# A squared-ReLU MLP's down pass: four row operands with stored low parts, four loaded later, one block between sum and square

## The chip, the cores and the metric

The kernel runs on one core of a Trainium2 chip. The metric is device time in microseconds (us) of one execution, and the number reported is the median of several runs. In what follows PE is TensorE, DVE is VectorE, ACT is ScalarE, POOL is GpSimd and SP is SyncE. SP and POOL each issue DMA transfers here, in the order in which they stand in that engine's program.

## The reference, cut to what matters

One layer of a decoder with attention, a convolution module and an MLP is computed for 512 prompt rows and 64 sample rows, 576 rows in all. The change lies in the MLP and touches its neighbours:

```
x    = x + concat(attn, conv) @ w_out                 # 2048 features
hid  = square(relu(rms_norm(x, g_mlp) @ w_up))        # 2048 -> 8192
x    = x + hid @ w_down                               # 8192 -> 2048
gate = sigmoid(rms_norm(x, g_ple) @ w_ple_gate)       # 2048 -> 2048
y    = rms_norm(x + (pe @ w_ple) * gate, g_final)
```

All of it is float32, with each row's norm taken over its 2048 features. The sum over the 8192 hidden features in `hid @ w_down` may be taken in any order.

## The kernel before

**Two stages.** The first, some 1000 us, computes the input projection, attention, convolution and output projection (`phase1`, the matmuls of line 493). The second is `phase2`, which works through three products one after another: the *up pass* (g = 1, `w_up`), the *down pass* (g = 2, `w_down`) and the *gate* (g = 3 to 5, `w_gate`). Features lie on partitions and rows on the free axis. A *row group* is 256 features of all 576 rows, so the input of the up pass and of the gate has 8 row groups and the hidden layer has 32.

**A block.** The up and down passes use a seven-product scheme for 2x2 blocks: a row group is kept as seven half-width operands (288 rows each; three are pieces of the data, four are sums `T` of them), a weight block as seven 128x128 operands, and seven products in seven PSUM banks are combined into a result afterwards. Each operand is split into a high part in the fast float32 type and a low part, the rest; each product then takes three matmuls (lines 1547 to 1549: high by high, high by low, low by high). So one *block*, one row group against one *part* of 256 output features, is 21 matmuls. The up pass has 32 parts of 8 blocks (blocks 0 to 255), the down pass 8 parts of 32 blocks (256 to 511). The down pass cuts each part's 32 blocks into several rounds: the first round takes the first 3, 3, 3, 4, 5, 6, 7 and 8 row groups for parts 0 to 7 (`DOWN_FIRST`), and each later round 7 or fewer. A part that isn't in its last round is added to DRAM by an accumulating DMA (line 1363).

**Row operands.** They live in a ring of eight slots (`xs`), each with seven high and seven low operands. When the last block that uses a slot is emitted, `mk` (line 1459) makes the next one: `load` issues on POOL's queue the DMA of the 1008 KB that a row group has in DRAM (`down_in`, in traces `di`, for the down pass; line 1470), and `build` then splits it in the slot: ACT copies it to the high part (`split_hi`, line 149), DVE subtracts (`split_lo`, line 152), in two pieces of 128x864 and 128x1152. All eight slots of the up pass are used until its last part, so slots 0 to 7 of the down pass are made during blocks 247 to 254 and first used in blocks 256, 257, 258, 268 (the last one of the fourth part's first round), 273, 279, 286 and 294. In the gate a slot holds row groups in another form, split by lines 1484 to 1486 (`xs<-xs,vecs`).

**Weights.** SP loads two blocks' weights in 512 KB (`w2r`, four buffers). For each block DVE forms sums of them (lines 1770 to 1772), ACT makes the high part (`w2h`, line 149) and DVE the low part (`w2l`, line 152), two blocks ahead of PE, with three buffers each.

**The end of a part.** ACT and DVE empty the seven banks and combine them (`combine_head`, lines 1663 to 1666, and `combine_tail`, lines 1676 to 1679). Then a generator finishes the part: `fin_up` multiplies by the row norm's scale on DVE, takes relu and square on ACT (lines 1354, 1355), forms the sums `T` on DVE and stores the row group to `down_in` on POOL's queue (lines 1311 to 1313); `fin_down` adds a partial part to DRAM or, in a part's last round, adds the residual on DVE (line 1366), stores it, and has ACT square it (line 1280) and DVE add the squares up for the next norm (line 1287). After the last part `norm` sums over partitions on PE (line 179), runs a chain of short DVE operations to 1/sqrt, puts them on a diagonal (`dg`, lines 183 and 185), spreads them by PE (line 189) and copies them to `rb` on ACT (line 190).

**What sets the order.** Each engine executes its instructions in the order in which the program emits them. The generators (finishing of parts in queue 0, builds of slots in queue 1, the last up part's finish in queue 2) are held by `Beside`. After each block `run` lets them emit as much as fits in the block's 2.79 us by their own estimate: a generator yields the cost of what it emitted, or a negative number, -n, to be passed over for n blocks. `flush` emits what is left of a generator at once where its result is needed. So a `yield -1` between two lines sets in the program one more block's weight work between the two, on every engine. Buffers of tag `b` (128 x 1152, `buf`, line 1268) hold `T`, squares, residuals and the diagonal; there are two of them.

## Time and profile before

| | |
|---|---|
| median of 3 runs | 2713.27 us (2712.22 to 2721.72) |
| profiled execution | 2715.1 us, span 2713.3 us |
| PE busy | 2658.0 us, 98% of the span, 21873 matmuls |
| DVE busy | 2044.1 us, 75% |
| ACT busy | 1151.2 us, 42% |
| POOL busy | 513.5 us, 19% |
| DMA | 536.12 MB, mean 198 GB/s |

The profiled execution took 2715.1 us from the host's view and 2713.3 us between its first and last record, so 1.8 us lie around the span. It is within the three runs' range. In the profile, the first matmul of the up pass starts at 1016.2 us of the span, the first of the down pass at 1742.8 us and its last at 2481.8 us; the gate follows. PE's busy time counts a matmul from its start to its modelled end, and matmuls overlap; what tells whether PE lost time in a stretch is the number of matmuls that it started there. The granted clock beside a stretch is 1.00 where PE had its full clock.

### The profile page before, as it was taken

The page shows a single profiled execution, that of the slowest core. Times are in us where ns is not written, and L with a number is a line of the kernel's source. Part 1 is how long each engine was busy: PE and PEld are TensorE (multiplying, and loading weights), DVE is VectorE, ACT ScalarE, POOL GpSimd, SP SyncE. Part 2 cuts the span into 40 slices and gives each one's busy share as a digit, 9 for nine tenths or more (in the row PEclk, how much of TensorE's full clock was granted, in tenths as well). Part 3 has the DMA queues.
Part 4 walks back from the last instruction along what each step waited for, and adds up shares of the span by engine and source line. Part 5 has one row for each costly group of instructions (what it writes and reads, how often), then busy time and mean ns, then how long its engine had stood idle before and what let it go on. Part 6 is the DMA issues. An engine that isn't in the chain of part 4 may idle for free.

```text
span 2713.3 us, 56293 instructions
## 1 busy us (share of the span) xinstructions
PE 2658.0 (98%) x21873; PEld 2569.6 (95%) x21873; DVE 2044.1 (75%) x3553; ACT 1151.2 (42%) x1692; POOL 513.5 (19%) x906
## 2 busy tenths in 40 slices
PE   9999999999999999999999999999999999998997
PEld 8899999888989998999999999999999999998997
DVE  6577777646554448888888888898888888897676
ACT  5222232235443325444444444454444444444554
POOL 2287786611000000000000000100000000000110
PEclk9999999999999999999999999999999999999998
DMA  5598898899754545444444444666565656655675
GB/s 203 176 302 295 299 297 294 286 308 319 242 202 149 175 168 171 155 142 142 142 140 141 142 143 140 233 149 174 164 189 155 182 154 179 177 183 186 192 241 172
DMA packets 238382, 536.12 MB, mean 198 GB/s; under 512 B 25537, under 2 KB 26562, under 8 KB 238114
## 3 DMA queue, kind: packets, MB, share of 16 engines
q1 hardware_dynamic: 170978, 327.86, 38.0%
q0 software_dynamic: 33600, 143.70, 16.9%
q10 hardware_dynamic: 33536, 60.96, 6.8%
q8 instruction: 171, 2.80, 0.4%
q14 instruction: 97, 0.79, 0.1%
HBM read 441.47 MB, written 90.96 MB: 196 GB/s over the span
## 4 chain that ended last, share of the span: by engine, by line
PE 55%; DVE 3%; issue 1%; ACT 1%; DVEq 0%; ACTq 0%
PE P L1548 16%; PE P L1547 16%; PE P L1549 16%; PE P L1616 2%; PE P L1617 2%; PE P L1615 2%; DVE w2l L152 1%; ACT w2h L149 0%; DVE xs L152 0%; DVE w2r L1771 0%; DVE w2r L1770 0%; DVE w2r L1772 0%; DVE x L1603 0%; DVE c L1664 0%; DVE c L1679 0%
## 5 line engine op out<-in xcount | busy, mean ns | idle before, releaser
L1547 PE MATMUL P<-xs,w2h 128*128 128x288 f32 x3584 | 1063.0, 297 | 11.8 <-DVE c L1664 8.3
L1548 PE MATMUL P<-xs,w2h 128*128 128x288 f32 x3584 | 1063.8, 297 | 4.7 <-DVE xs L152 4.7
L1549 PE MATMUL P<-xs,w2l 128*128 128x288 f32 x3584 | 1061.0, 296 | 2.0 <-DVE w2l L152 2.0
L149 ACT ACTIVATE w2h<-w2r 128x896 fp32r<-128x896 f32 (+1 forms) x632 | 556.7, 889 | 740.7 <-PE P L1548 450.7
L152 DVE TENSOR_TENSOR w2l<-w2r,w2h 128x896 fp32r<-128x896 f32 (+1 forms) x632 | 638.4, 1012 | 224.3 <-ACT w2h L149 220.8
L1547 PEld LDWEIGHTS P<-xs,w2h 128*128 128x128 f32 x3584 | 676.3, 189 | 16.9 <-DVE c L1664 10.5
L1548 PEld LDWEIGHTS P<-xs,w2h 128*128 128x128 f32 x3584 | 676.5, 189 | 7.3 <-DVE xs L152 7.0
L1549 PEld LDWEIGHTS P<-xs,w2l 128*128 128x128 f32 x3584 | 674.1, 188 | 3.8 <-DVE w2l L152 3.6
L493 PE MATMUL U<-xh,whi 128*128 128x288 f32 x1792 | 399.4, 304 | 0.0
L493 PE MATMUL U<-xl,whi 128*128 128x288 f32 x1792 | 383.1, 295 | 1.0 <-DVE xl L331 1.0
L493 PE MATMUL U<-xh,wlo 128*128 128x288 f32 x1792 | 383.5, 296 | 0.0
L493 PEld LDWEIGHTS U<-xh,whi 128*128 128x128 f32 x1792 | 286.9, 189 | 18.6 <-issue 16.3
L123 ACT ACTIVATE whi<-wraw 128x512 fp32r<-128x512 f32 x224 | 140.7, 629 | 356.0 <-PE U L493 321.0
L493 PEld LDWEIGHTS U<-xl,whi 128*128 128x128 f32 x1792 | 288.1, 188 | 1.9 <-DVE xl L331 1.9
L493 PEld LDWEIGHTS U<-xh,wlo 128*128 128x128 f32 x1792 | 288.0, 188 | 0.0
L129 DVE TENSOR_TENSOR wlo<-wraw,whi 128x512 fp32r<-128x512 f32 x224 | 159.8, 715 | 114.3 <-ACT whi L123 114.0
L1040 DVE SCALAR_TENSOR_TENSOR y<-ue,cv,y 128x512 f32<-128x512 f32 x240 | 184.1, 767 | 5.3
L1770 DVE TENSOR_TENSOR w2r<-w2r 128x512 f32<-128x512 f32 (+1 forms) x273 | 178.0, 652 | 5.4 <-DMA w2r<-in_w_down 5.4
L1041 POOL TENSOR_SCALAR cvt<-us,cv 128x64 f32<-128x64 f32 x240 | 165.5, 690 | 22.3
L1616 PE MATMUL P<-xs,w2h 128*128 128x288 f32 x512 | 151.7, 296 | 1.7 <-DVE xs L1486 1.7
L1615 PE MATMUL P<-xs,w2h 128*128 128x288 f32 x512 | 152.0, 297 | 1.4 <-ACT xs L149 1.4
L1617 PE MATMUL P<-xs,w2l 128*128 128x288 f32 x512 | 151.7, 296 | 1.1 <-DVE w2l L152 1.0
(382 smaller groups left out, 2759.0 us busy)
## 6 DMA issues: line engine op xcount, KB each, us to landing
k<-in_cache_kv SPq DMA_DIRECT2D x256, 256.0 KB, 4.8
v<-in_cache_kv SPq DMA_DIRECT2D x256, 256.0 KB, 4.8
w2r<-in_w_up SPq DMA_DIRECT2D x127, 512.0 KB, 4.0
w2r<-in_w_down SPq DMA_DIRECT2D x112, 512.0 KB, 3.9
wraw<-in_w_main ACTq DMA_DIRECT2D x156, 256.0 KB, 5.0
xs<-di POOLq DMA_DIRECT2D x32, 1008.0 KB, 6.1
w2r<-in_w_gate SPq DMA_DIRECT2D x60, 512.0 KB, 4.5
x<-c POOLq DMA_DIRECT2D x48, 576.0 KB, 6.4
```

The source lines that it names most:

```text
L149: self.nc.scalar.activation(out, in_, AF.Copy, **kw)
L152: self.nc.vector.tensor_tensor(out, in_, f(hi), ALU.subtract)
L493: self.nc.tensor.matmul(u[:, r, :HR], w, x[:, r * HR:(r + 1) * HR], start=first and n == 0, stop=last and n == 2)
L1040: nc.vector.scalar_tensor_tensor(y, ue[:, j:j + NPR], w, y, ALU.mult, ALU.add)
L1041: nc.gpsimd.tensor_scalar(t, us[:, :, j:j + 8], w, None, ALU.mult)
L1547: nc.tensor.matmul(o, hi[:, ia, :], s.hi[:, ib, :], start=(i == 0), stop=False)
L1548: nc.tensor.matmul(o, hi[:, ia, :], s.lo[:, ib, :], start=False, stop=False)
L1549: nc.tensor.matmul(o, lo[:, ia, :], s.hi[:, ib, :], start=False, stop=(i == n - 1))
L1615: nc.tensor.matmul(o, hi[:, ia, :], s.hi[:, kh, rows], start=first and kh == 0, stop=False)
L1616: nc.tensor.matmul(o, hi[:, ia, :], s.lo[:, kh, rows], start=False, stop=False)
L1617: nc.tensor.matmul(o, lo[:, ia, :], s.hi[:, kh, rows], start=False, stop=last and kh == 1)
L1770: lambda: V(w[:, :, 4:6, :], w[:, :, 0:1, :].broadcast_to([128, m, 2, 128]), w[:, :, 1:3, :], ALU.add),
```

## The change

There are five edits, all in the second stage.

1. *Order of the hidden features.* The down pass takes row groups 8, 9, 10 and 11 first, then 0 to 7, then 12 to 31 (`DOWN_K`). `w_down` is reordered on the host to match. Slot number j now holds row group `DOWN_K[j]`.
2. *Stored low parts.* When parts 8 to 11 of the up pass are finished, `low_rows` also makes the low part of their seven operands (ACT's copy to the high type and DVE's subtraction, once for the four sums and once for the three pieces) and stores it to DRAM (`down_lo`, in traces `dl`). Slots 0 to 3 of the down pass then get two loads, the data into the high place and the stored low part into the low place; the split that is left is ACT's copy in place.
3. *Late loads.* Slots 3 to 7 (from `DOWN_FIRST[0]` = 3 up to the ring's eight) issue their loads in `build`, not when the ring has room, and `build` is passed over until 11 blocks ahead of the slot's first use. (Slot 3 is both: its low part is stored and its loads are late.)
4. *One block between DVE's result and ACT.* `fin_up` yields -1 after DVE's multiplication, ahead of relu and square, and `fin_down` yields -1 after DVE's addition, ahead of the square, in the last round of each part.
5. *Buffers of tag `b`*: three in place of two.

```diff
@@ -30,6 +30,8 @@
 DOWN_FIRST = (3, 3, 3, 4, 5, 6, 7, 8)
 DOWN_PART = 7
 RING = 8
+READY = 4
+DOWN_K = (*range(8, 8 + READY), *range(8), *range(8 + READY, 32))
 OUT_ORDER = (0, 1, 4, 5, 6, 7, 2, 3)
 
 
@@ -224,6 +226,7 @@
             self.up_in = [dram.tile([128, 7, HR], F32, name=f"ui{j}") for j in range(8)]
             self.qd = [dram.tile([128, NPR], F32, name=f"qd{j}") for j in range(8)]
             self.down_in = [dram.tile([128, 7, HR], F32, name=f"di{j}") for j in range(32)]
+            self.down_lo = {j: dram.tile([128, 7, HR], F32R, name=f"dl{j}") for j in DOWN_K[:READY]}
             cst = top.enter_context(tc.tile_pool(name="cst", bufs=1))
             self.ones = cst.tile([128, 128], F32, name="ones")
             nc.gpsimd.memset(self.ones, 1.0)
@@ -1266,7 +1269,7 @@
 
 
     def buf(self, name):
-        return self.t2.tile([128, 2, NR], F32, name=name, tag="b", bufs=2)
+        return self.t2.tile([128, 2, NR], F32, name=name, tag="b", bufs=3)
 
     def pairbuf(self, src):
         r = self.buf("rp")
@@ -1311,6 +1314,27 @@
         nc.gpsimd.dma_start(dst[:, 0, :], c[:, 0, :HR])
         nc.gpsimd.dma_start(dst[:, 1:3, :].rearrange("p a n -> p (a n)"), c[:, 1, :])
         nc.gpsimd.dma_start(dst[:, 3:, :], T)
+
+    def low_rows(self, c, T, dst):
+
+        nc = self.nc
+        four = lambda: self.buf("lr").rearrange("p a (b n) -> p (a b) n", b=2).bitcast(F32R)
+        lo = four()
+        self.split_hi(lo, T)
+        yield -2
+        self.split_lo(lo, T, lo)
+        nc.gpsimd.dma_start(dst[:, 3:, :], lo)
+        yield EL(2 * NR)
+        yield -1
+        lo = four()
+        b2 = c[:, 1, :].rearrange("p (a b) -> p a b", a=2)
+        self.split_hi(lo[:, 0, :], c[:, 0, :HR])
+        self.split_hi(lo[:, 1:3, :], b2)
+        yield -2
+        self.split_lo(lo[:, 0, :], c[:, 0, :HR], lo[:, 0, :])
+        self.split_lo(lo[:, 1:3, :], b2, lo[:, 1:3, :])
+        nc.gpsimd.dma_start(dst[:, :3, :], lo[:, :3, :])
+        yield EL(3 * HR)
 
     def fin_out(self, p, c):
         nc = self.nc
@@ -1351,11 +1375,14 @@
         def fin_up(p, c, r, final):
             V(c, c, rbb, ALU.mult)
             yield EL(2 * NR)
+            yield -1
             nc.scalar.activation(c, c, AF.Relu)
             nc.scalar.activation(c, c, AF.Square)
             yield -1
             c, T = yield from self.operands(c, None)
             self.stored(c, T, self.down_in[p])
+            if p in self.down_lo:
+                yield from self.low_rows(c, T, self.down_lo[p])
 
         def fin_down(p, c, r, final):
 
@@ -1366,6 +1393,7 @@
             V(c, c, r, ALU.add)
             yield EL(2 * NR)
             nc.gpsimd.dma_start(self.x2[p], c)
+            yield -1
             yield from self.squares(p, c)
             if p == 7:
                 bg.add(0, self.norm(self.P_))
@@ -1464,18 +1492,36 @@
             else:
                 t = self.xslot()
                 h.hi, h.lo = t[:, 0], t[:, 1]
-            src = (self.up_in, self.down_in, self.x2)[g - 1][j]
+            n = DOWN_K[j] if g == 2 else j
+            src = (self.up_in, self.down_in, self.x2)[g - 1][n]
+            ready, late = g == 2 and j < READY, g == 2 and DOWN_FIRST[0] <= j < RING
+
             def load():
-                bg.flush(fin_of[g - 1, j])
-                nc.gpsimd.dma_start(f(h.lo), src)
-
-            if g < 3:
+                bg.flush(fin_of[g - 1, n])
+                if ready:
+                    nc.gpsimd.dma_start(f(h.hi), src)
+                    nc.gpsimd.dma_start(h.lo, self.down_lo[n])
+                else:
+                    nc.gpsimd.dma_start(f(h.lo), src)
+
+            if g < 3 and not late:
                 load()
 
             def build():
-                if g == 3:
+                if late:
+                    yield min(bg.now - 1000 - firstuse[2, j] + 11, -1)
+                if g == 3 or late:
                     load()
-                yield (-2, -3, -4)[(g == 2 and j >= RING) + 2 * (g == 3)]
+                if ready:
+                    yield -3
+                    for i, m in ((0, 3), (3, 7)):
+                        self.split_hi(h.hi[:, i:m, :], f(h.hi[:, i:m, :]))
+                        yield -1
+                    return
+                if late:
+                    yield -3
+                else:
+                    yield (-2, -3, -4)[(g == 2 and j >= RING) + 2 * (g == 3)]
                 if g < 3:
                     yield from self.slot(t)
                     return
@@ -1489,10 +1535,11 @@
             h.work = bg.add(1, build())
 
         quadlist = [(si, k) for si, ks in enumerate(self.orders) for k in ks]
-        lastuse, seg0 = {}, {}
+        lastuse, seg0, firstuse = {}, {}, {}
         for t, (si, k) in enumerate(quadlist):
             lastuse[min(segs[si][0], 3), k] = t
             seg0.setdefault(si, t)
+            firstuse.setdefault((min(segs[si][0], 3), k), t)
         lastseg = {sg[:2]: si for si, sg in enumerate(segs)}
         segend = {si: t for t, (si, k) in enumerate(quadlist)}
         hooks = {}
@@ -1836,7 +1883,7 @@
     wo = g["w_out"][0].reshape(8, 2, 128, 16, 128)[list(OUT_ORDER)].reshape(16, 128, 16, 128)
     d["w_out"] = C(wo.transpose(2, 1, 0, 3))
     d["w_up"] = quads(g["w_up"][0], 32, 8)
-    d["w_down"] = quads(g["w_down"][0], 8, 32)
+    d["w_down"] = np.ascontiguousarray(quads(g["w_down"][0], 8, 32)[:, :, list(DOWN_K)])
     d["w_gate"] = quads(g["w_ple_gate"][0], 8, 8)
 
     d["w_ple"] = C(g["w_ple"][0].reshape(2, 128, 4, 4, 128).transpose(2, 1, 3, 0, 4).reshape(4, 128, 8, 128))
```

POOL's queue at the hand-over from the up pass to the down pass, before. `di_113` to `di_120` are row groups 0 to 7 that are loaded into slots 0 to 7; `di_143` and `di_144` are the stores of row groups 30 and 31; `x_0` to `x_5` are the partial parts of the first round that are added to DRAM.

```order
L1470 DMA xs<-di_113 128x2016
L1470 DMA xs<-di_114 128x2016
L1470 DMA xs<-di_115 128x2016
L1311 DMA di_143<-c 128x288
L1312 DMA di_143<-c 128x576
L1313 DMA di_143<-T 128x1152
L1470 DMA xs<-di_116 128x2016
L1470 DMA xs<-di_117 128x2016
L1470 DMA xs<-di_118 128x2016
L1470 DMA xs<-di_119 128x2016
L1470 DMA xs<-di_120 128x2016
L1363 DMA x_0_81<-c 128x1152
```

The same queue after, from the third part's write on; ahead of these rows stand the six loads of slots 0 to 2, the stores of `di_143` and `di_144` and the writes of `x_0` and `x_1`. `di_124` and `dl_148` are slot 3's data and its stored low part, `di_113` to `di_117` are slots 4 to 7 and the slot after them.

```order
L1390 DMA x_2_83<-c 128x1152
L1502 DMA xs<-di_124 128x2016
L1503 DMA xs<-dl_148 128x2016
L1390 DMA x_3_84<-c 128x1152
L1505 DMA xs<-di_113 128x2016
L1390 DMA x_4_85<-c 128x1152
L1505 DMA xs<-di_114 128x2016
L1390 DMA x_5_86<-c 128x1152
L1505 DMA xs<-di_115 128x2016
L1505 DMA xs<-di_116 128x2016
L1505 DMA xs<-di_117 128x2016
L1390 DMA x_6_87<-c 128x1152
```

All eight loads stood ahead of the first part's write; now the first six do, and each later one stands behind the write of a part.

ACT at the hand-over, before: the copies of slots 0, 1 and 2 (`xs<-xs`), of the weights (`w2h`), and the emptying of the last two up parts and the first down part (L1663, L1666).

```order
L149 ACTIVATE xs<-xs 128x864
L149 ACTIVATE xs<-xs 128x1152
L149 ACTIVATE w2h<-w2r 128x896
L1663 ACTIVATE c<-P 128x288
L1666 ACTIVATE t_22159<-P 128x288
L149 ACTIVATE w2h<-w2r 128x896
L149 ACTIVATE xs<-xs 128x864
L149 ACTIVATE w2h<-w2r 128x896
L149 ACTIVATE xs<-xs 128x1152
L149 ACTIVATE w2h<-w2r 128x896
L1663 ACTIVATE c<-P 128x288
L1666 ACTIVATE t_22265<-P 128x288
```

And after:

```order
L151 ACTIVATE w2h<-w2r 128x896 x2
L1710 ACTIVATE c<-P 128x288
L1713 ACTIVATE t_22195<-P 128x288
L151 ACTIVATE w2h<-w2r 128x896
L151 ACTIVATE xs<-xs 128x864
L151 ACTIVATE xs<-xs 128x1152
L151 ACTIVATE w2h<-w2r 128x896
L151 ACTIVATE xs<-xs 128x864
L151 ACTIVATE xs<-xs 128x1152
L151 ACTIVATE w2h<-w2r 128x896
L1710 ACTIVATE c<-P 128x288
L1713 ACTIVATE t_22301<-P 128x288
```

Two slots' copies now stand between the emptying of the last up part and that of the first down part, each with both pieces in a row; before it was one slot's, with a weight copy between its pieces.

ACT near the end of the down pass, before: `sq` is the square of a finished part (L1280), `xs<-xs,vecs` builds rows of the gate.

```order
L1663 ACTIVATE c<-P 128x288
L1666 ACTIVATE t_29835<-P 128x288
L149 ACTIVATE w2h<-w2r 128x896
L1280 ACTIVATE sq_29883<-c 128x1152
L149 ACTIVATE w2h<-w2r 128x896
```

And after:

```order
L1710 ACTIVATE c<-P 128x288
L1713 ACTIVATE t_29875<-P 128x288
L151 ACTIVATE w2h<-w2r 128x896
L151 ACTIVATE xs<-xs,vecs 128x576
L151 ACTIVATE w2h<-w2r 128x896
L1283 ACTIVATE sq_29951<-c 128x1152
```

The square stands behind one more weight copy, and a piece of the gate's rows comes ahead of it.

DVE behind the last down part, before: the end of the norm's chain (`rrt` to `dg`), then the weights' low parts (`w2l`) and the gate's rows.

```order
L168 TENSOR_TENSOR rrt<-rrs 128x5
L169 TENSOR_SCALAR rrt<-rrt,rrm 128x5
L170 TENSOR_SCALAR rrs<-rrt,rrs 128x5
L183 TENSOR_TENSOR dg<-ident,rrs 128x512
L185 TENSOR_SCALAR dg<-ident,rrs 128x64
L152 TENSOR_TENSOR w2l<-w2r,w2h 128x512
L1486 TENSOR_SCALAR xs<-xs,vecs 128x576 x2
```

And after:

```order
L170 TENSOR_TENSOR rrt<-rrs 128x5
L171 TENSOR_SCALAR rrt<-rrt,rrm 128x5
L172 TENSOR_SCALAR rrs<-rrt,rrs 128x5
L185 TENSOR_TENSOR dg<-ident,rrs 128x512
L187 TENSOR_SCALAR dg<-ident,rrs 128x64
L1532 TENSOR_SCALAR xs<-xs,vecs 128x576 x2
L154 TENSOR_TENSOR w2l<-w2r,w2h 128x512
```

The chain now stands one block later: a slot's rows (`xs<-xs,vecs`) follow it directly, where a block's weight work came between.

## The prediction

> **What bounds the kernel now.** I read the page's totals first, then busy time by stretches of 100 us, then stretches of 10 us around the two places where TensorE issues less, then the waits there, and last each engine's timeline.
>
> ```profile
> PE 2658.0 (98%) x21873; PEld 2569.6 (95%) x21873; DVE 2044.1 (75%) x3553; ACT 1151.2 (42%) x1692; POOL 513.5 (19%) x906
> 1600.00:1700.00 100.00, 100.00 (x752) 100.00 (x751) 84.89 (x135) 46.34 (x54) 6.45 (x12) 1.00 0.46 143
> 1700.00:1800.00 100.00, 93.14 (x671) 90.80 (x670) 89.70 (x144) 48.66 (x59) 12.70 (x21) 0.98 0.69 214
> 1800.00:1900.00 100.00, 98.37 (x740) 97.74 (x740) 88.94 (x138) 48.73 (x58) 6.00 (x8) 1.00 0.59 161
> 2400.00:2500.00 100.00, 94.44 (x686) 92.54 (x685) 85.63 (x147) 44.50 (x60) 6.92 (x13) 0.98 0.58 196
> 2500.00:2600.00 100.00, 96.23 (x706) 94.72 (x707) 62.87 (x103) 53.25 (x92) 9.30 (x14) 0.98 0.62 190
> ```
>
> Columns of the stretches: length, then busy us and count for PE, PEld, DVE, ACT, POOL, then granted clock, DMA share, GB/s. TensorE is the bound: at its pace it starts 752 matmuls in 100 us, 0.133 us each, so a block (one slot of rows, 21 matmuls) lasts 2.79 us. Only missing matmuls cost time. From 1700 to 1900 (up pass into down pass) 81 + 12 = 93 are missing, 12.4 us; from 2400 to 2600 (down pass into gate) 66 + 46 = 112, 14.9 us, part of it the norm's own matmuls. That is all this change can win back: 27 us, 1.0%. In 1600:1700 the up pass loses nothing.
>
> ```profile
> 1740.00:1750.00 10.00, 9.25 (x67) 1.00 1.00 406
> 1750.00:1760.00 10.00, 6.88 (x37) 0.83 0.59 212
> 1790.00:1800.00 10.00, 10.00 (x78) 1.00 0.62 120
> 2440.00:2450.00 10.00, 9.63 (x72) 1.00 0.43 152
> 2450.00:2460.00 10.00, 7.68 (x53) 1.00 0.61 201
> 2460.00:2470.00 10.00, 9.75 (x75) 1.00 0.49 152
> 2470.00:2480.00 10.00, 7.77 (x44) 0.83 0.54 179
> PE P L1547 <- DVE c L1664: 3.6, 4, 1.3
> PE P L1547 <- ACT xs L149: 2.0, 1, 2.0
> PE P L1548 <- DVE xs L152: 1.6, 2, 1.1
> PE P L1547 <- ACT c L1663: 1.3, 3, 0.6
> ```
>
> Here PE alone is shown, with its clock, DMA share and GB/s; 78 starts fill 10 us. The four waits are those of 1740 to 1810: a slot's split by ScalarE and VectorE comes late (xs), and VectorE empties a finished part's banks late (c). In the stretches with clock 0.83 a stall also halved the clock: 17% of 10 us, 1.7 us.
>
> **The change, part by part.** *Slots 0 to 3, low parts stored.* VectorE's split of a slot leaves the hand-over four times:
>
> ```profile
> 1740.62 2.32 DVE L152 TENSOR_TENSOR xs<-xs 128x864 fp32r<-128x864 f32 x2
> 1744.45 0.91 ACT L149 ACTIVATE xs<-xs 128x864 fp32r<-128x864 f32 x1
> 1751.23 1.15 ACT L149 ACTIVATE xs<-xs 128x1152 fp32r<-128x1152 f32 x1
> 1757.97 0.95 ACT L149 ACTIVATE w2h<-w2r 128x896 fp32r<-128x896 f32 x1 [1.36 <-PE P L1548]
> ```
>
> 4 x 2.32 = 9.3 us of VectorE work, at a place where it is the late engine. It is paid in the up pass: per stored row group one 128x1152 subtraction and two smaller ones, as long as one split, 2.3 us on VectorE, some 2.1 us on ScalarE, and two DMA issues on GpSimd. VectorE's 84.89% of a 22.3 us part is 18.9 us; with 2.3 more it is 21.2, so it fits with 1 us to spare. Four such parts: I take 0.5 us; bounds 0, and 4 x 2.3 = 9 if none hides.
>
> Six loads of 1008 KB for slots 0 to 2 now start where the first three stood. At 406 GB/s less the weights' 512 KB per two blocks (94 GB/s) one takes 3.3 us, so with the next row group's store (also 1008 KB) the sixth lands some 2 + 7 x 3.3 = 25 us after the first issue (1723.65, below), at 1749. Slot 0 is used at 1743 and slot 2 at 1749, so they are just in time. ScalarE's copies of slots 1 and 2 stand between the weight copies of neighbouring blocks (0.95 + 0.91 + 1.15 = 3.0 us in a row against a block of 2.79), and the one for slot 2 waits first for VectorE's weight sums: 1.0 us late, bounds 0 and the 2.0 us of the row `ACT xs` above.
>
> Between parts, PE still waits for ScalarE and VectorE to empty the banks, since the relu and square of the last but one up part stand in front of the copies as before: rows c, 3.6 + 1.3 = 4.9 us before; I step through the same rows with the splits gone and get 1.6 and 2.0.
>
> *Slot 3, and slots 4 to 7, loaded later.* GpSimd's order decides: slot 3's two loads stand behind the write of the third down part, slot 4's behind the fourth, slot 5's behind the fifth, slots 6 and 7's behind the sixth.
>
> ```profile
> 1723.65 0.54 POOL L1470 DMA_DIRECT2D xs<-di  x1 [13.04 <-PE P L1549]
> 1782.72 0.86 POOL L1363 DMA_DIRECT2D x<-c  x1 [6.52 <-DVE c L1679]
> 1787.54 0.95 ACT L149 ACTIVATE w2h<-w2r 128x896 fp32r<-128x896 f32 x1 [1.60 <-PE P L1548]
> xs<-di POOLq DMA_DIRECT2D x8, 1008.0 KB, 10.7
> x<-c POOLq DMA_DIRECT2D x6, 576.0 KB, 5.6
> ```
>
> The second row is the write in question; it waits for VectorE to finish that part. The third is ScalarE released by the end of the block ahead of slot 3's first use: 4.8 us after the write began (5.2 by my steps, where VectorE is less behind). The write lands after 5.6 us (last row), and behind it on the same queue the two loads need 3.3 us each: 12.2 us. So the block that uses slot 3 waits 12.2 - 5.2 = 7.0 us for the low part, and such a stall halves the clock: 1.7 more, 8.7 in all. Bounds: 0 if both loads overtake the write and share its 5.6 us; 10.7 (row of eight loads in one run) x 2 - 5.2 = 16 at worst. I take 8.7, since the queue in this stretch holds nothing but these three.
>
> Slots 4 and 5 are copied by ScalarE directly after the weights of the block behind their first use, so w2h 0.95, copies 0.91 and 1.15, then VectorE's second half 1.35 follow each other, some 4.4 us, from the start of the block before; PE wants the last piece after 2.79 + 0.5 us: about 1.3 us late, twice, 2.7 with rounding. Slots 6 and 7 have three blocks and more: 0.
>
> Hand-over after: 1.0 + 1.6 + 2.0 + 8.7 + 2.7 = 16.0, against 12.4: **+3.6 us.**
>
> *One block between VectorE's sum and ScalarE's square, down pass.*
>
> ```profile
> 2446.20 1.17 ACT L1280 ACTIVATE sq<-c 128x1152 f32<-128x1152 f32 x1 [4.94 <-DVE c L1366]
> 2447.28 0.94 ACT L149 ACTIVATE w2h<-w2r 128x896 fp32r<-128x896 f32 x1
> 2448.24 1.09 DVE L152 TENSOR_TENSOR w2l<-w2r,w2h 128x896 fp32r<-128x896 f32 x1 [1.87 <-ACT w2h L149]
> PE P L1549 <- DVE w2l L152: 1.7, 3, 0.7
> PE P L1547 <- DVE c L1664: 3.2, 2, 2.2
> ```
>
> ScalarE stood 4.94 us at the square, with the next block's weight copy queued behind it, VectorE then waited 1.87 us for that copy, and PE for VectorE (last two rows, 2440 to 2530). Now that copy goes first. From 2440 to 2480 6 + 25 + 3 + 34 = 68 starts are missing, 9.0 us with the halved clock; I keep 1.5 and 1.2 at the ends of two short parts and 0.2 at a weight, and some 0.4 that the norm's shift may take: **-5.7 us.**
>
> *The norm behind it.* The last square is one block later, and with it PE's row sums and the matmul that spreads the scale.
>
> ```profile
> 2494.99 1.17 PE L179 MATMUL P<-ones,acc 128*128 128x2 f32 x10
> 2496.20 0.17 DVE L181 TENSOR_SCALAR rrm<-P 128x5 f32<-128x5 f32 x1 [2.92 <-PE P L179]
> 2499.22 0.25 DVE L185 TENSOR_SCALAR dg<-ident,rrs 128x64 f32<-128x64 f32 x1
> 2499.99 1.54 DVE L1486 SCALAR_TENSOR_TENSOR xs<-xs,vecs 128x576 fp32r<-128x576 f32 x2
> 2505.07 0.60 ACT L190 ACTIVATE rb<-P 128x512 f32<-128x512 f32 x1 [5.07 <-PE P L189]
> 2500.00:2510.00 10.00, 7.33 (x42) 0.93 0.33 113
> ```
>
> VectorE's chain from the row sums (2496.20 to 2499.5) stands ahead of the low part of gate slot 5. Before, a whole block ran on PE meanwhile and PE still waited 1.5 us. After, slot 5's block follows the row sums directly: 3.3 for the chain, 0.1 for the wait, 0.75 for the first low part, 4.2 us of stall and 1.7 of clock. ScalarE's copy of the scale (5.07 us of waiting) moves from slot 6's copies to slot 7's, where it leaves 2.0. That is 7.9 against 1.5 + 1.9 + 1.5 before (36 starts missing in the last row, less the norm's own 1.0 us): **+3.0 us.**
>
> *Without a price.* In the up pass the relu and square move behind one more weight copy; PE loses nothing there, and the 15% of VectorE that is idle covers it. A third buffer of tag b removes waits of loads only, none of which PE sees. The reordered w_down lies the same way in memory.
>
> **A rule weighed.** PE's longest wait in 1740 to 1760 was 2.0 us, and the clock still halved. The Trainium skill, TensorE: Matmul & The Clock Gate, part 1, says the gate halves after at least one idle window of about 3.4 us. By that rule only the stalls of 7.0 and 4.2 us pay 1.7 us, which is the sum as it stands. By the row the two stalls of 2.0 us may pay it as well, 3.4 us more. I keep the smaller, since three other waits of 1 to 2 us in these rows left the clock at 1.00.
>
> **Sum.** +0.5 + 3.6 - 5.7 + 3.0 = +1.4 us. The profiled execution took 2715.1 us (span 2713.3); it becomes 2716.5. Against the median of the three runs, 2713.27, that is 2714.7.
>
> **Rivals.**
> 1. *Slot 3 is not late.* If its loads land with the write, 8.7 us go: 2706.0; if the norm's stall is also only as before, 2703. For it: eight loads in a row did keep PE fed for four slots; against it: GpSimd's order. This reaches below 2699.7 (0.5%) only if the part ends go too.
> 2. *Slower by over 0.5%: the GpSimd queue holds up every late slot.* Place: slots 4 to 7, whose loads stand behind the writes. A load is issued about 2 us after its part ends, lands some 9.8 us after that end by the same 5.6 + 3.3, and ScalarE reaches it after about 9.3. Each further us is a us of stall, since ScalarE's next weight copies wait behind it. If writes take 9 us instead of 5.6, slots 4, 5 and 6 lose 3.4 us and 1.7 of clock each, 15 us: 2730. It decides from a landing 12.5 us after the part's end. Against it: the median 5.6.
> 3. *The stored low parts do not fit in the up pass*: none of the 9 us hides: 2723.
> 4. *The moved square brings nothing*, since VectorE itself is the late engine at the ends of the short parts: the 5.7 us stay: 2720.
>
> **How the numbers follow.** Forecast as summed 0.47 (its own range 2709 to 2720), rival 1 0.22, rival 2 0.09, rival 3 0.11, rival 4 0.11. The range reaches to rival 1's 2703 and rival 3's 2723, rounded up by the second 1.7 us of clock to 2725. 0.5%, 13.6 us, is about what a measurement of this kernel can tell from no change; the runs of before span 9.5 us. Faster than 2699.7: the tail of rival 1, 0.07. Slower than 2726.8: rival 2, 0.09. The rest, 0.84, within.
>
> **What the profile after would show.** Right: no DVE split of slots 0 to 3; PE's longest wait of the hand-over at the block of slot 3, released by a DMA or by ScalarE's copy of it, 5 us or more; clock below 1.00 there; 750 starts or more in 100 us up to 1700; no wait of w2l behind a square from 2440 to 2480; the wait for gate slot 5 at 4 us. Wrong: slot 3's block without a wait, waits in the up pass's last parts, or the waits at part ends grown.

## The result and the profile after

In 20 runs of each kernel the changed one took 2723.18 us (median; 2712.14 to 2727.64) and the one before 2715.11 us (2704.35 to 2724.93). The ratio is 1.0036 (95% interval 1.0026 to 1.0047), so the change costs about 9.8 us by the ratio (the two medians differ by 8.1); +1.4 us was forecast. The profiled execution has a span of 2722.5 us.

The page's totals of the changed kernel:

```profile
PE 2661.1 (98%) x21873; PEld 2570.0 (94%) x21873; DVE 2043.6 (75%) x3557; ACT 1159.6 (43%) x1704; POOL 520.4 (19%) x918
```

Its busy time by stretches of 100 us, with the columns of the prediction's rows:

```profile
1200.00:1300.00 100.00, 98.49 (x732) 96.84 (x732) 87.73 (x137) 50.58 (x63) 9.14 (x17) 1.00 0.51 161
1600.00:1700.00 100.00, 100.00 (x761) 100.00 (x760) 86.15 (x136) 46.35 (x54) 6.65 (x13) 1.00 0.46 146
1700.00:1800.00 100.00, 89.28 (x647) 87.78 (x646) 78.62 (x132) 47.18 (x57) 13.35 (x22) 0.97 0.69 215
1800.00:1900.00 100.00, 96.59 (x702) 95.01 (x701) 86.98 (x134) 47.75 (x57) 7.61 (x11) 0.98 0.63 185
2400.00:2500.00 100.00, 98.12 (x728) 96.92 (x727) 90.55 (x143) 47.38 (x63) 6.92 (x13) 1.00 0.61 204
2500.00:2600.00 100.00, 93.25 (x665) 91.53 (x664) 60.02 (x107) 49.96 (x85) 9.28 (x14) 0.95 0.58 184
```

The first of these stretches in the kernel before, which the prediction did not show:

```profile
1200.00:1300.00 100.00, 100.00 (x753) 100.00 (x751) 84.98 (x134) 46.05 (x54) 6.44 (x12) 1.00 0.44 137
```

Four things moved. 1200 to 1300, where the stored low parts are made, now loses 21 starts. The hand-over (1700 to 1900) loses 62 more starts than before. The end of the down pass gains 42. The norm and the gate (2500 to 2600) lose 41. A fifth was not looked for: in 1600 to 1700, where nothing waits, PE starts 761 matmuls where it started 752 before.

To set these side by side I add up, from the starts of the matmuls in each trace, every distance between two starts of over 0.16 us, less the usual 0.133 us, and call the sum of a stretch its *stall* (halved clock included). Each kernel was profiled twice:

| stretch | before, us | after, us | change forecast | change measured |
|---|---|---|---|---|
| start of the up pass (blocks 0 to 31) | 9.3, 9.0 | 8.3, 8.3 | 0 | -0.9 |
| stored row groups (blocks 85 to 110) | 0.0, 0.0 | 5.1, 5.4 | +0.5 | +5.3 |
| hand-over (blocks 250 to 309) | 13.6, 13.2 | 21.7, 20.3 | +3.6 | +7.6 |
| middle of the down pass | 1.7, 1.1 | 3.0, 2.8 | 0 | +1.5 |
| end of the down pass (blocks 490 to 511) | 8.6, 7.3 | 3.3, 3.8 | -5.7 | -4.4 |
| norm and gate (60 us from there) | 7.8, 7.8 | 13.0, 11.0 | +3.0 | +4.2 |
| sum | | | +1.4 | +13.3 |

That is 3.5 us more than the runs' 9.8, and 5.9 more than the 7.4 by which the spans of the two profiled pairs differ. The pace of PE and a later start of the up pass, both below, account for all but 0.4 of the latter.

*The stored low parts.* (PE stalls at three of the four row groups; the one made first costs it nothing.) ScalarE's and VectorE's timeline of the changed kernel at one of the four row groups (start, duration, and in brackets the idle time before with what ended it):

```profile
1263.70 1.17 ACT L151 ACTIVATE lr<-T 128x1152 fp32r<-128x1152 f32 x1 [2.81 <-DVE T L1681]
1264.78 1.77 ACT L151 ACTIVATE w2h<-w2r 128x896 fp32r<-128x896 f32 x2
1265.74 1.09 DVE L154 TENSOR_TENSOR w2l<-w2r,w2h 128x896 fp32r<-128x896 f32 x1 [1.47 <-ACT w2h L151]
```

The waits of ScalarE and of PE there, from 1250 to 1330 (total us, times, longest):

```profile
ACT lr L151 <- DVE T L1681: 8.4, 3, 2.8
PE P L1596 <- DVE w2l L154: 1.8, 3, 0.6
```

ScalarE stands 2.81 us at the copy of `T` with the next weight copy queued behind it; VectorE waits 1.47 us for that copy, PE for VectorE. The 1.8 us count only the time in which PE was idle; since matmuls overlap, part of each gap between starts does not show as idle, and the gaps make 5.1. It is the kind of wait that the change takes out of the down pass's end, made anew in the up pass.

*The hand-over.* GpSimd's, ScalarE's and PE's timeline of the changed kernel at slots 3 and 4:

```profile
1775.66 0.88 POOL L1390 DMA_DIRECT2D x<-c  x1 [3.61 <-DVE c L1726]
1776.23 0.88 POOL L1502 DMA_DIRECT2D xs<-di  x1
1776.77 0.88 POOL L1503 DMA_DIRECT2D xs<-dl  x1
1784.20 1.98 ACT L151 ACTIVATE xs<-xs 128x864 fp32r<-128x864 f32 x2 [5.32 <-DMA xs<-di]
1785.18 0.40 PE L1594 MATMUL P<-xs,w2h 128*128 128x288 f32 x1 [4.60 <-ACT xs L151]
1786.09 0.93 ACT L151 ACTIVATE w2h<-w2r 128x896 fp32r<-128x896 f32 x1
1787.41 0.61 PE L1595 MATMUL P<-xs,w2h 128*128 128x288 f32 x1 [1.83 <-DMA xs<-dl]
1802.70 1.98 ACT L151 ACTIVATE xs<-xs 128x864 fp32r<-128x864 f32 x2 [0.52 <-DMA xs<-di]
1804.58 0.94 ACT L151 ACTIVATE w2h<-w2r 128x896 fp32r<-128x896 f32 x1
```

PE alone by 10 us in the same stretch (last columns: clock, DMA share, GB/s):

```profile
1780.00:1790.00 10.00, 3.57 (x17) 0.79 0.80 283
1790.00:1800.00 10.00, 10.00 (x68) 0.87 0.57 137
1800.00:1810.00 10.00, 8.62 (x50) 0.83 0.56 205
```

Slot 3's data lands 8.0 us and its low part some 11 us after their issue, behind the write; PE waits 4.60 and 1.83 us. At slot 4 (1802.70) ScalarE reaches the copy 0.52 us before the data, and the weight copy stands behind it. ScalarE's copies of slots 5 and 6:

```profile
1822.16 1.97 ACT L151 ACTIVATE xs<-xs 128x864 fp32r<-128x864 f32 x2
1840.07 1.98 ACT L151 ACTIVATE xs<-xs 128x864 fp32r<-128x864 f32 x2 [2.24 <-DMA xs<-di]
```

Slot 5's data is there in time; slot 6's keeps ScalarE waiting for 2.24 us. PE does not wait for slot 6 itself, but 1.0 us in the block behind it (287, the first of a part) for VectorE to empty a bank (`c`, L1711): VectorE, with slot 6's split done late, works from 1841.02 to that emptying at 1849.80 with one pause of 0.55 us. The clock rows make 2.1 + 1.3 + 1.7 = 5.1 us of halved clock, where before it was 1.7 from 1740 to 1810.

*The norm.* PE's longest wait behind it, from the changed kernel's timeline:

```profile
2506.92 0.61 PE L1663 MATMUL P<-xs,w2h 128*128 128x288 f32 x1 [3.85 <-DVE xs L1532]
```

And PE by 10 us:

```profile
2500.00:2510.00 10.00, 6.15 (x38) 0.80 0.33 107
2510.00:2520.00 10.00, 8.20 (x44) 0.84 0.43 165
2520.00:2530.00 10.00, 10.00 (x68) 0.84 0.33 96
```

PE waits 3.85 us for gate slot 5 behind the norm's chain, and the clock is halved for 2.0 + 1.6 + 1.6 = 5.2 us' worth of work.

### The profile page after: what moved, and what is told of

It is laid out like the page before. It is cut to its first block, busy times and chain, and to the rows that moved or that the text cites. A ratio compares the mean times of both kernels' runs of the same rounds, so it can differ in the third digit from the quotient of the medians.

```text
span 2722.5 us, 56345 instructions
## 1 busy us (share of the span) xinstructions
PE 2661.1 (98%) x21873; PEld 2570.0 (94%) x21873; DVE 2043.6 (75%) x3557; ACT 1159.6 (43%) x1704; POOL 520.4 (19%) x918
## 5 line engine op out<-in xcount | busy, mean ns | idle before, releaser
L1044 POOL TENSOR_SCALAR cvt<-us,cv 128x64 f32<-128x64 f32 x240 | 164.8, 687 | 22.3
L1663 PE MATMUL P<-xs,w2h 128*128 128x288 f32 x512 | 153.0, 299 | 4.3 <-DVE xs L1532 4.3
```

The source lines that it names most:

```text
L1044: nc.gpsimd.tensor_scalar(t, us[:, :, j:j + 8], w, None, ALU.mult)
L1663: nc.tensor.matmul(o, hi[:, ia, :], s.lo[:, kh, rows], start=False, stop=False)
```

## The experiments

Stalls in us of the profiled execution of each, and its ratio to the kernel before timed beside it. The column "stored" holds all stalls of blocks 32 to 249; in the changed kernel all of these lie in blocks 85 to 110. (Of the two kernels profiled again, there is one run each, 2710.57 and 2716.11 us; the ratio in the second row is that of the 20 runs.)

| kernel | start | stored | hand-over | middle | end | gate | ratio (95% interval) |
|---|---|---|---|---|---|---|---|
| before, profiled again | 9.0 | 0.0 | 13.2 | 1.1 | 7.3 | 7.8 | |
| changed, profiled again | 8.3 | 5.4 | 20.3 | 2.8 | 3.8 | 11.0 | 1.0036 (1.0026 to 1.0047) |
| changed, slot 3 early | 8.3 | 5.3 | 15.8 | 3.0 | 3.3 | 12.5 | 1.0009 (0.9996 to 1.0023) |
| changed, no slot late | 8.4 | 5.4 | 6.4 | 1.0 | 3.8 | 10.9 | 0.9987 (0.9976 to 0.9999) |
| changed, no stored low parts | 8.3 | 0.0 | 26.3 | 1.6 | 3.4 | 10.6 | 1.0015 (0.9999 to 1.0031) |
| changed, low parts a block later | 8.3 | 1.3 | 20.7 | 2.8 | 3.7 | 10.6 | 1.0033 (1.0022 to 1.0044) |
| changed, norm as before | 8.3 | 5.3 | 24.0 | 3.2 | 3.4 | 7.8 | 1.0031 (1.0018 to 1.0044) |
| changed, relu as before | 9.2 | 8.6 | 16.7 | 2.8 | 3.8 | 12.7 | 1.0045 (1.0029 to 1.0061) |
| before, moved square only | 9.1 | 0.0 | 13.5 | 1.2 | 3.6 | 7.8 | 0.9977 (0.9962 to 0.9992) |
| before, moved relu only | 8.3 | 0.0 | 10.6 | 1.7 | 9.0 | 7.8 | 0.9966 (0.9951 to 0.9981) |
| before, late loads only | 9.1 | 0.0 | 21.0 | 1.1 | 8.5 | 7.8 | 1.0019 (1.0004 to 1.0033) |
| best of the parts | 8.3 | 1.5 | 8.1 | 1.3 | 3.7 | 6.3 | 0.9954 (0.9938 to 0.9971) |

**Both kernels again: the pace.**

> The kernel before, profiled once more. In the two profiles at hand a block of 21 matmuls that waits for nothing lasts either 2.80 us or 2.77 us, and which of the two holds changes only where PE has stalled; before had 2.80 in nearly all of the up pass, after 2.77 in nearly all of it, worth some 7 us. Theory 1 (the pace is drawn anew in every execution): the stretches at 2.77 lie elsewhere than in the first profile of this kernel, while the matmul starts missing at stalls stay within 1 us of 13.3 us at the hand-over, 8.6 us at the end of the down pass and 7.7 us at the norm. Theory 2 (the pace belongs to the program): blocks 32 to 254 are at 2.80 again.

> The changed kernel, profiled once more. Theory 1 (pace drawn anew): the stretches at 2.77 us a block lie elsewhere than in its first profile; the stalls stay within 1 us of 5.1 us at the four stored row groups, 21.7 us at the hand-over, 3.3 us at the end of the down pass, 13.0 us at the norm. Theory 2 (pace belongs to the program): blocks 106 to 255 are at 2.77 again, and the change gains some 7 us by it in each run.

One stretch of the up pass, PE alone, in the second profile of the kernel before:

```profile
1500.00:1600.00 100.00, 100.00 (x752) 1.00 0.46 144
```

The same in the second profile of the changed kernel:

```profile
1500.00:1600.00 100.00, 100.00 (x762) 1.00 0.45 139
```

Neither theory held whole. A block that waits for nothing lasts 2.80 or 2.77 us, and the pace changes only at a wait. In the up pass before had none of blocks 32 to 254 at 2.77, twice; the changed kernel 204 and 209, twice: that speaks for the program. In the down pass the changed kernel had 11 and then 206: that speaks for the run. The other profiles show where the program comes in. The five of kernels without the moved relu (before twice, the moved square, the late loads, the relu put back) all have a small wait in block 29 and 2.80 us behind it. The nine with it have none there; behind their last wait, in block 24, six run at 2.77 us up to the next wait and three at 2.80. So, as far as 14 profiles tell, the moved relu leaves the up pass a chance of the faster pace, 0.033 us in each of up to 223 blocks, 7 us. With it the sum closes: stalls +13.3, pace in the up pass -6.8 (206 blocks), in the down pass -2.2 (68 blocks more, mean of two), and a start of the up pass 3.5 us later (1017.9 and 1019.8 against 1016.2 and 1014.4) make 7.8; the spans of the two pairs differ by 7.4. The later start is not shown to be an effect of the change: no edit stands in the first stage, and over the 14 profiles that start lies anywhere from 1014.4 to 1025.1 us. What sets the pace was not tried.

**Slot 3 early, and no slot late.**

```diff
-            ready, late = g == 2 and j < READY, g == 2 and DOWN_FIRST[0] <= j < RING
+            ready, late = g == 2 and j < READY, g == 2 and READY <= j < RING
```

> The changed kernel with slot 3's two loads issued when the ring has room, as those of slots 0 to 2; only slots 4 to 7 are late. My theory (ScalarE waits 5.3 us for slot 3's data with the next weight copy queued behind it, PE then for both and the clock halves): the stall at block 267 and 268 of 9.3 us goes, the hand-over falls from 21.7 to 12 or 13 us, and the time is 8 to 9 us below the changed kernel's, ratio 1.000 to the kernel before. Rival (the two loads only shift the congestion: eight loads at once delay slots 0 to 2): the stalls before 1765 grow by 4 us or more, ratio 1.002 or more.

```diff
-            ready, late = g == 2 and j < READY, g == 2 and DOWN_FIRST[0] <= j < RING
+            ready, late = g == 2 and j < READY, False
```

> The changed kernel with no slot late: all eight slots load when the ring has room, slots 0 to 3 with their stored low parts, 12 loads in all. Theory (lateness is the cost; the stored low parts take work off VectorE): with slot 3's stall the ones in blocks 273, 279 and 287 go too, hand-over 11 to 12 us (15.8 with slot 3 alone early), ratio 1.000. Rival (12 loads at once are too many, the weights or slots 1 and 2 come late): hand-over 16 us or more, ratio 1.001 or more.

PE's waits of the hand-over (1740 to 1860) in the changed kernel:

```profile
PE P L1594 <- ACT xs L151: 5.9, 3, 4.6
PE P L1595 <- DVE xs L154: 2.4, 4, 0.7
PE P L1595 <- DMA xs<-dl: 1.8, 1, 1.8
```

With slot 3 early:

```profile
PE P L1594 <- ACT xs L151: 2.8, 4, 1.2
PE P L1595 <- DVE xs L154: 2.8, 4, 0.7
```

With no slot late:

```profile
PE P L1594 <- DVE c L1711: 1.8, 2, 1.5
PE P L1594 <- ACT c L1710: 1.4, 1, 1.4
PE P L1594 <- ACT xs L151: 1.2, 2, 0.8
```

With slot 3 early its 9.2 us vanish, but slots 4 to 6 then cost 10 instead of 6.6, so the hand-over falls by 5.2 only, not 8 to 9. With no slot late it falls to 6.4, far under the 11 to 12 expected: lateness as a whole costs 15 us, and twelve loads in a row hold nothing up. The ratio turns below 1. This is one profile of each; the 15 us stand well clear of the 20.3 to 24.0 us that the hand-over takes in four profiles where its program is that of the changed kernel.

**No stored low parts.**

```diff
-READY = 4
-DOWN_K = (*range(8, 8 + READY), *range(8), *range(8 + READY, 32))
+READY = 0
+DOWN_K = tuple(range(32))
```

> The changed kernel without stored low parts and without the new order of the hidden features: slots 0 to 3 are loaded once and split in the slot by ScalarE and VectorE as before; slots 3 to 7 are still late. My theory: the 5.1 us at the stored row groups go (none of it was in the kernel before), slots 0 to 2 get their VectorE splits back and cost some 3 us more before 1765, and slot 3 has one load of 1008 KB less in front, which takes 3 us off its stall: about 5 us below the changed kernel, ratio 1.0015 to 1.002. Rival (the stored low parts earn their price at the hand-over): the hand-over grows by 5 us or more and the ratio is 1.0035 or more.

The stored row groups' stall is gone, as it should be, but the hand-over rises by 5.3 us to 26.3, the rival's figure. Some 3 us of that stand in blocks 257 and 258, where VectorE's splits are back (5.4 for 1.9), as my theory had it; but slot 3's stall stays (9.0 for 9.2) with one load less in front, which it had wrong. By the stalls, then, the stored low parts earn at the hand-over with late loads what they cost in the up pass. The timed ratio, 1.0015, is the theory's, and the rival's 1.0035 lies outside its interval; since that interval overlaps the changed kernel's, it stays open whether this kernel is the faster one. Without late loads the hand-over is 6.4 for 13.4 before. The moved relu alone makes 2.8 of these 7.0 us, and the 4.2 left, if the parts add up, are less than the 5.3 that the stored low parts cost as the change makes them.

**Low parts a block later.**

```diff
         nc = self.nc
+        yield -1
         four = lambda: self.buf("lr").rearrange("p a (b n) -> p (a b) n", b=2).bitcast(F32R)
```

> The changed kernel with one block's weight work put between VectorE's sums T and ScalarE's copy of them in the making of the stored low parts. Theory: ScalarE waits 2.81 us for T with the next weight copy queued behind it, VectorE and PE then for that copy; with the block in between, the 5.1 to 5.4 us at the four stored row groups fall to 1.5 or less and nothing else moves, ratio to before about 1.002 (the changed kernel 1.0036). Rival (VectorE and ScalarE simply have no room for the added work in a part of 22 us): 4 us or more stay there.

The stall falls from 5.3 to 1.3 us, with the same work on VectorE: it was the order, not the room. In this kernel ScalarE's waits at the same place read:

```profile
ACT w2h L151 <- PE P L1596: 20.6, 16, 1.9
ACT lr L151 <- DVE T L1682: 1.8, 1, 1.8
```

It mostly waits for PE now, and for `T` 1.8 us once, where the changed kernel's row above has 8.4 us in three. The ratio, 1.0033, is hardly lower than the changed kernel's, and the 1.002 expected lies just below its interval; the 4 us show in the trace but not in the time.

**The norm as before.**

```diff
             nc.gpsimd.dma_start(self.x2[p], c)
-            yield -1
+            if p < 7:
+                yield -1
             yield from self.squares(p, c)
```

> The changed kernel with the block between sum and square left out for the last part alone, so that its square and the norm stand where they stood before. Theory (the norm one block later is what costs at the gate): stalls at the gate fall from 11 to 13 us to the 7.8 us of before, those at the end of the down pass stay at 3.3 to 3.8, ratio about 1.002. Rival (the cost at the gate comes from the square of the last part itself or from the gate's slots, whatever the norm does): the gate stays at 11 us or more, ratio 1.0035.

The gate returns to 7.8 us and the end of the down pass stays at 3.4: the place of the last part's square and of the norm behind it, which the edit moves back together, is the cost. The ratio 1.0031 shows little of it, and this profile's hand-over was 24.0 us, some 3 us longer than in the two of the changed kernel, though nothing differs there in the program; a late load's price varies from run to run by as much.

**The relu as before, and the moved relu alone.** The first is the changed kernel without the `yield -1` of `fin_up`, the second the kernel before with it.

```diff
             V(c, c, rbb, ALU.mult)
             yield EL(2 * NR)
+            yield -1
             nc.scalar.activation(c, c, AF.Relu)
```

> The changed kernel without the block between VectorE's multiplication and ScalarE's relu in the up pass. Theory (no price): the stalls of the up pass proper stay at 5.1 to 5.4 us, all of it at the stored row groups; at the start of the up pass 0.8 us come back (9.2 for 8.3); the hand-over within 2 us of 21; ratio 1.003 to 1.004. Rival (the moved relu is what makes the stored row groups stall, because it pushes T and so the low parts behind): the 5 us fall below 2, ratio 1.002 or less.

> The kernel before with one edit alone: one block between VectorE's multiplication and ScalarE's relu in the up pass. Theory from the run without this block (the hand-over fell from 21 to 16.7 us): the block puts relu and square of the last two parts in front of the copies and bank emptying of the first down parts, hand-over 17 to 18 us for 13.4, the start of the up pass 8.3 for 9.1, ratio 1.001 to 1.002. Rival (no price by itself, only together with the stored low parts and the late loads): hand-over 12.5 to 14.5 us, ratio 0.999 to 1.000.

The first gave a hand-over of 16.7 us, and from that I expected the block to cost 4 us at the hand-over by itself. It does the opposite: alone it takes 2.8 us off, so that the cost of 4 us shows only together with late loads and stored low parts; by what path was not traced. The moved relu also kept 3.3 us off the stored row groups (5.3 against 8.6). Alone it is worth 0.0034 of the time, 9 us, more than its stalls (0.9 + 2.8, less 1.1 at the end of the down pass). The pace may be the rest, but that is not shown: its one profile ran the up pass at 2.80.

**The moved square alone, parts 0 to 6.**

> The kernel before with one edit alone: one block between VectorE's sum and ScalarE's square in the down pass, parts 0 to 6 only, the last part as it was. Theory: the end of the down pass falls from 7.3 to 8.6 us of stalls to 3.5, hand-over (13.4) and gate (7.8) stay, so 4 to 5 us are gained, ratio 0.998. Rival (the end of the down pass is limited by VectorE and the stall returns at the next part): the three together fall by less than 2 us, ratio 0.9995 or more.

PE's waits from 2440 to 2480 in this kernel, beside the rows w2l 1.7 and c 3.2 of before:

```profile
PE P L1549 <- DVE c L1666: 1.6, 2, 1.0
PE P L1551 <- DVE w2l L152: 0.4, 1, 0.4
```

The end of the down pass falls to 3.6 us, nothing comes back later, and the ratio is 0.9977: this part of the change is a gain.

**Late loads alone.** The kernel before with slots 3 to 7 late, two buffers of tag `b`, no stored low parts and no moved relu or square.

> The kernel before with one edit alone: slots 3 to 7 load late (11 blocks ahead of their first use), each with its one load of 1008 KB and the split of both parts in the slot. Theory (the load that stands behind a part's write lands after ScalarE has reached its copy, with the weight copies queued behind it): a stall of 4 us or more in blocks 267 and 268 and smaller ones in 273, 279 and 287; the hand-over 19 us or more for 13.4, ratio 1.002 or more. Rival (one load without the stored low part behind it is in time): hand-over 15 us or less, ratio 1.000.

The hand-over rises from 13.4 to 21.0 us, 7.6, and the kernel is slower by 0.0019. The wait at slot 3 is smaller with one load (blocks 267 and 268 last 3.98 and 4.79 us, 7.56 and 7.20 in the changed kernel), slot 4's is larger (blocks 272 and 273: 5.49 and 6.17, for 2.86 and 6.32). So the theory's hand-over and ratio came out, but not its place: the larger stall was expected at slot 3.

**The best of the parts.** The changed kernel with no slot late, the low parts a block later, the norm as before, and the moved relu for parts 0 to 29 only.

```diff
-            yield -1
+            if p < 30:
+                yield -1
             nc.scalar.activation(c, c, AF.Relu)
```

> The changed kernel with what the runs so far point to: no slot late, one block between T and the making of the stored low parts, the block ahead of relu left out for the last two up parts, the block ahead of the square left out for the last down part. Theory (each cost stands by itself): up pass 1.3 us, hand-over 8 to 9, end of the down pass 3.5, gate 7.8, in all 5 us below the kernel before with the moved square alone, ratio 0.996. Rival (what the stored low parts save at the hand-over is no more than what they cost in the up pass): hand-over 12 us or more, ratio 0.998 or more, no better than the moved square alone.

It is 0.0046 faster than the kernel before, 12.5 us, and 0.8% faster than the change as made. The hand-over, 8.1 us, is as expected but no better than without the exception for the last two parts (6.4), which brought nothing that one profile each could show. Its busy time by stretches of 100 us:

```profile
1700.00:1800.00 100.00, 95.06 (x699) 93.03 (x697) 86.02 (x142) 53.11 (x66) 14.81 (x25) 1.00 0.79 263
2500.00:2600.00 100.00, 98.88 (x749) 98.41 (x747) 64.42 (x107) 57.09 (x98) 11.36 (x16) 1.00 0.65 207
```

These are its stretches of the hand-over's first half and of the norm. The clock stays whole in both, where the changed kernel had 0.97 and 0.95. The name goes too far, though. The moved relu alone and the moved square alone measured 0.9966 and 0.9977; if the two add up they make 0.9943, without stored low parts, and that lies within this kernel's interval. The two together were not run, so nothing here shows that stored low parts are worth having. The new order of the features and the third buffer of tag `b` were not tried by themselves either.

## Why the prediction was right and where it was wrong

The time, 2723.18, lies in the range of 2703 to 2725, near its upper end, and 9.8 us is within the 0.5% called no change. That it stays in the range is in part luck: the stalls, +13.3 us, would have made it 2728.4, and the pace, which the prediction did not know, took some 9 off in the profiled pairs. Of the signs that it listed, two failed: 1200 to 1300 has 732 starts where 750 or more were expected, and PE's longest wait of the hand-over is 4.60 us, not 5 or more. The terms of the sum fared as follows.

- *The stored low parts, +0.5:* mis-sized, +5.3. The working counted VectorE's room (18.9 us of a part of 22.3) and found it enough. It was enough; the run with one more block between shows 1.3 us with the same work. What failed was to treat a cost as hidden by room without asking what stands behind the new instructions: ScalarE's copy waits for `T` with the weights' copy queued. This is rival 3's place at a bit over half its price, by another mechanism.
- *Part ends and slots 1 and 2, 4.6:* blocks 262 and 265 lose 3.7 us (1.6 + 2.0 forecast), blocks 257 and 258 1.9 (1.0).
- *Slot 3, 8.7:* 9.2 in blocks 267 and 268, with the place, the two releasers and the landing (the write's 5.6 and two loads of 3.3) as worked out. The waits were 6.4 us for 7.0; the clock was halved for two windows of 3.41 us where one was counted, and made the other 2.8 for 1.7.
- *Slots 4 to 7, 2.7:* mis-sized, 6.6 (blocks 273, 279 and 287 last 6.3, 4.4 and 4.2 us). The waits for VectorE's second halves of slots 4 and 5 came as forecast: 2.4 us, the row `DVE xs` above, though the working's own figures (4.36 less 3.29) make 1.1 each and not 1.3. Two things were left out: slot 4's wait halved the clock for a window, and slot 6, put at nothing, cost 1.4 us through the bank that VectorE emptied late. Rival 2's mechanism, with a chance of 0.09, is in this in small: ScalarE waits 0.5 us for slot 4's data and 2.2 for slot 6's, none for slot 5's.
- *The moved square, -5.7:* right in mechanism; -4.4, since one of the two profiles of before had 7.3 us there to lose and not 8.6. Rival 4 fell.
- *The norm, +3.0:* right in place, releaser and wait (3.85 us for 4.2); +4.2, since the clock was halved for three windows (two in the second profile) rather than one. The figure for before was also too high by its own row: 36 starts less the norm's 1.0 us make 3.8 us and not 4.9.
- *The moved relu, without a price:* wrong. It takes 0.9 us off the start and, with no slot late, 2.8 off the hand-over, and it leaves room for the faster pace in the up pass.
- *The middle of the down pass* was not in the sum: +1.5.
- *Rival 1*, that slot 3 is not late, is refuted by the trace, and its run shows that there was less to win than 8.7.

So the forecast's side of the 0.5% was right, but its sum, +1.4, stands 8.4 us below the 9.8, mostly for two terms that it had too small by 4 to 5 us each, and 12 us below the stalls; the pace hid part of that.

*The rule on the clock.* Of the two readings weighed, the one kept gave the right price for the two stalls at part ends (blocks 262 and 265, 1.7 and 1.9 us, left the clock whole), but as a rule the row's was the better. The clock in the records changes only on a grid of 3.41 us. From 1000 us on in six profiles (both kernels twice, the moved square, no slot late) I worked out PE's busy share in each such window from the matmul records: all ten windows below 0.45 were followed by a halved one, 9 of 22 between 0.46 and 0.61, and one of all those above 0.62: a window that was itself at half clock, 0.75 busy, behind the norm in the changed kernel. The window of slot 4's wait in the changed kernel was 0.60 busy and was followed by a halved one. The Trainium skill, TensorE: Matmul & The Clock Gate, part 1, has the window of about 3.4 us, free-running, which these traces bear out; they differ from its condition of one idle window, since a window that was about half idle was enough in part of the cases here.

## What to carry to other kernels

An instruction that waits costs what is queued behind it on its engine: before adding work to an engine with room, look for the operand it waits for and put a step of the steady work in between; one `yield` took 4 us off PE's stalls here, twice. A load moved later costs more than the wait for its own data when it stands behind a write and when its consumer shares an engine with the steady work; here twelve early loads beat both mixtures tried. A change of several parts is best timed part by part: this one held a gain of 7 us and a loss of 15 us in the hand-over alone, and a gain of 4 in the down pass.

## What the runs showed of the hardware

PE has two paces for one and the same stream of matmuls at full granted clock: 2.80 us a block (133.3 ns a matmul) and 2.77 (131.75 ns), 752 or 761 in the profile's rows of 100 us. It holds one until a wait, however small, after which it may hold the other; over phase 2 that is up to 17 us (512 blocks of 0.033), as much as most effects measured here, and it belongs to the spread between runs of one kernel (20.6 us for the kernel before). Its cause is open. And waits well below a window of 3.41 us can halve the clock (before, 2.0 us at the hand-over did): 9 of 22 windows that were 0.46 to 0.61 busy were followed by a halved one.
